# Another order for the first two tiles' work, half of each weight guard from VectorE's maxima, and the third tile transposed by DMA

## The chip, the cores and the metric

The kernel runs on one core of a Trainium2 chip. The metric is the device time of one execution in microseconds; the median of the runs counts. TensorE multiplies matrices, VectorE, ScalarE and GpSimd (POOL in the rows) do the elementwise work, and SyncE (SP) issues most DMA transfers.

## What is computed

One layer of an encoder on 4096 tokens of width 1024. The input is normalized, projected to eight groups of 512 columns (four for a gated convolution; q, k, v and a gate z for dilated window attention with eight heads), and the joined result goes through an output projection:

```python
h = rmsnorm(x, norm_w)
proj = jnp.einsum('bsd,de->bse', h, w_in)            # (4096 x 1024) @ (1024 x 4096)
u, g_b, g_c, z_conv, q, k, v, z_attn = jnp.split(proj, splits, axis=-1)
y_conv = short_gated_conv(u, g_b, g_c, conv_w, conv_b) * jax.nn.silu(z_conv)
q, k = rmsnorm(q, q_norm_w), rmsnorm(k, k_norm_w)    # per head of 64
for window, dilation in ((128, 1), (512, 4), (2048, 16)):
    o_i, lse_i = dilated_window_attention(q, k, v, rel_bias, window, dilation)
y_attn = sum(softmax(lses) * outs) * jax.nn.silu(z_attn)
x = x + jnp.concatenate([y_conv, y_attn], -1) @ w_out
```

## The kernel before

Every float32 operand of a product is split into two float16 parts, hi and lo, and a product is three matmuls (hi by hi, hi by lo, lo by hi) of 128 x 512 outputs. The program is written for each engine as one queue, in the order of the code; each engine works its queue strictly from front to back and waits where an operand is late.

The kernel has three phases: projections of q, k, v and z for all 32 tiles of 128 tokens (phase A), attention interleaved with the convolution's projections (phase B), and the output projection. The change touches the head of phase A only.

**Weights.** Groups 4, 5, 6 and 7 of `w_in` are q, k, v and z. A group is eight pieces of 128 x 512 (`raw`), one per 128 rows, called kt 0 to 7. Before it can be split, a group needs a scale that keeps its float16 parts in range, its guard. `w_square` sums a piece's squares on ScalarE into one column of `wss`; `w_scale` adds the eight columns, adds over the partitions by a one-column matmul with `ones` on TensorE, takes the inverse root on GpSimd and writes the scales `nws` on VectorE. Then `w_split` writes hi on ScalarE and lo on VectorE, piece by piece, to `wa`.

**Tiles.** `stats1` and `stats2` give a tile's inverse root of the mean square (ScalarE's sum, GpSimd's power, a few one-column steps on VectorE). Tiles 0, 1 and 2 go through `x_transpose`: VectorE scales the tile, TensorE transposes it in eight blocks to two banks of PSUM, ScalarE writes hi and VectorE lo. From tile 3 on `x_split` writes the two parts untransposed, and two DMA transposes from SyncE's queue bring them to `hb`.

**Products.** `mm` runs one group for one tile or, for the first two tiles, for both together, 48 matmuls; its argument `between` names work that is queued behind the matmuls of a kt. In the head the calls are pq, pk, pv and pz (groups 4 to 7 for tiles 0 and 1), and between their matmuls stand the next group's guard and splits, the norms of q and k (`post_qk1` sums squares, `post_qk2` scales and splits), and `v_sums`: eight matmuls with `ones16` over the absolute values of v's hi weights, which give per-column scales that `post_v` and `post_z` need. After pz the steady loop starts with group 4 of tile 2, here called pq(2).

Of the kernel before, what the change touches and what calls it, by code (L numbers as in the profile page):

```python
# [65 lines left out]
def tile_hybrid_block(  # L66
# [193 lines left out]
    def w_scale(cg):  # L260
# [28 lines left out]
    def group_steps(cg):  # L289
        def spl(kt):  # L290
            w = wa[(cg - 4) * 8 + kt]
            w_split(w[:, 0], w[:, 1], raw.pop((cg, kt)), cg, kt)
        return ([lambda kt=kt: w_square(cg, kt, raw[cg, kt]) for kt in range(KT)], [lambda: w_scale(cg)],
                [lambda kt=kt: spl(kt) for kt in range(KT)])
# [49 lines left out]
    def h_views(t):  # L344
        c = t // 2
        b = (hb[c] if t % 2 else h_room(c, c % 3))[:, t % 2]
        HT[t] = (b[:, 0], b[:, 1])
        return HT[t]

    def x_transpose(t, b0=4):  # L350
        hi, lo = h_views(t)
        nc.vector.tensor_scalar(XT[t], XT[t], RX.pop(t), None, op0=OP.mult)
        for g in range(2):
            p = bank(b0 + g, [128, 4, 128])
            for k in range(4):
# [91 lines left out]

    def v_sums():
        pcs = bank(7, [128, 512])
        for n in range(KT):  # L450
            a = pa.tile([128, 512], F16, name="wk", bufs=3)
            nc.scalar.activation(a, wa[16 + n][:, 0], AF.Abs)
            nc.tensor.matmul(pcs, ones16, a, start=n == 0, stop=n == KT - 1)
        nc.vector.tensor_scalar(vinv, pcs, 1e-30, None, op0=OP.max)
# [54 lines left out]
    steps = {cg: group_steps(cg) for cg in (4, 5, 6, 7)}  # L509
# [3 lines left out]
    stats1(0)  # L513
    stats1(1)
    stats2(0)
    stats2(1)
    x_transpose(0, 4)
    x_transpose(1, 6)
    for part in steps[4]:
        run_tasks(part)  # L520

    def with_steps(cg, more=None):
        sq, fin, spl = steps[cg]
        out = {kt: [] for kt in range(KT)}
        for kt in range(4):
            out[kt] += sq[2 * kt:2 * kt + 2]
        out[3] += fin
        for kt in range(4):
            out[4 + kt] += spl[2 * kt:2 * kt + 2]
        for kt, tasks in (more or {}).items():  # L530
            out[kt] += tasks
        return out

    pq = mm((0, 1), 0, 4, with_steps(5), 4)
    pk = mm((0, 1), 2, 5, with_steps(6, {
        0: [lambda: post_qk1(0, "q", pq[0])], 1: [lambda: post_qk1(1, "q", pq[1])], 2: [gains],
        5: [lambda: post_qk2(0, "q")], 7: [lambda: post_qk2(1, "q")]}))
    pv = mm((0, 1), 4, 6, with_steps(7, {
        0: [lambda: post_qk1(0, "k", pk[0]), lambda: qk_store(0, "q")], 1: [lambda: post_qk1(1, "k", pk[1])],
        2: [lambda: qk_store(1, "q"), v_sums], 3: [lambda: stats1(2)], 4: [v_scales, lambda: stats2(2)],  # L540
        5: [lambda: post_qk2(0, "k"), lambda: x_transpose(2, 0)], 6: [lambda: post_qk2(1, "k")], 7: [v_gate]}))
    load_x(3)
    load_x(4)
    pz = mm((0, 1), 2, 7, {
        0: [lambda: qk_store(0, "k"), lambda: post_v(0, pv[0])], 1: [lambda: qk_store(1, "k"), lambda: post_v(1, pv[1])],
        2: [lambda: h_store(0), lambda: stats1(3)], 4: [lambda: stats2(3)]})
# [704 lines left out]
```

## Time and profile before

| what | value |
|---|---|
| median of 3 runs | 2262.62 us (2255.15 to 2264.13) |
| the profiled execution's own time | 2264.64 us |
| its span | 2262.8 us |
| TensorE busy | 2152.2 us, 95% of the span |
| VectorE, ScalarE, GpSimd busy | 1427.5, 1087.2, 769.4 us |

The span is the time from the first to the last instruction in the trace; the execution's own time is 1.8 us longer. Times in the rows below are counted from the span's start.

### The profile page before, as it was taken

How to read it: one execution, taken by the hardware profiler on the slowest of the kernel's cores; microseconds unless marked ns; L12 is line 12 of the kernel's file. 1: busy time of each engine (PE TensorE's matmuls, PEld its weight loads, DVE VectorE, ACT ScalarE, POOL GpSimd, SP SyncE). 2: the span in 40 equal slices, each digit the busy share in tenths (PEclk: the TensorE clock that was granted, in tenths of full speed). 3: DMA queues.
4: the chain of work that ended last, by engine and by line, in shares of the span. 5: the costliest groups of instructions: out<-in, count | busy, mean ns of one | idle time of the engine just before them, and what ended most of it. 6: DMA issues, size and time to landing. Idle time of an engine off the chain costs nothing. (4 is left out here: it accounts for less than half of the span.)

```text
span 2262.8 us, 48552 instructions
## 1 busy us (share of the span) xinstructions
PE 2152.2 (95%) x17726; PEld 1577.9 (70%) x17726; DVE 1427.5 (63%) x4009; ACT 1087.2 (48%) x3128; POOL 769.4 (34%) x1443
## 2 busy tenths in 40 slices
PE   5699999999999989999999999999999998999999
PEld 2244444444444778888888888888888897788887
DVE  4655665656656356766566666676666676787776
ACT  6423333333333156766566666666566675222221
POOL 1132332222233134533344323553233254343332
PEclk9899999999999999999999999999999999999999
DMA  5246467685655775689565896668966558587775
GB/s 178 77 133 169 151 169 171 171 202 144 165 164 142 176 149 134 139 168 191 135 153 116 177 183 153 143 157 170 177 149 132 134 116 223 188 258 257 237 239 188
DMA packets 625005, 377.83 MB, mean 167 GB/s; under 512 B 401281, under 2 KB 567292, under 8 KB 618620
## 3 DMA queue, kind: packets, MB, share of 16 engines
q1 hardware_dynamic: 503396, 304.19, 54.3%
q10 hardware_dynamic: 121368, 70.53, 12.2%
q8 instruction: 139, 2.28, 0.4%
q14 instruction: 102, 0.84, 0.1%
HBM read 174.54 MB, written 110.39 MB: 126 GB/s over the span
## 5 line engine op out<-in xcount | busy, mean ns | idle before, releaser
L809 PE MATMUL bank<-hb,w 128*128 128x256 f16 x2048 | 562.9, 275 | 0.1
L810 PE MATMUL bank<-hb,w 128*128 128x256 f16 x2048 | 560.2, 274 | 0.0
L811 PE MATMUL bank<-hb,w 128*128 128x256 f16 x2048 | 560.1, 274 | 0.0
L998 DVE CUSTOM_DVE_ANT_0 L<-bank,bt,alpha 128x256 f32<-128x256 f32 (+1 forms) x768 | 318.9, 452 | 135.3 <-PE bank L986 89.7
L387 PE MATMUL bank<-wa,hb 128*128 128x512 f16 x1024 | 392.0, 383 | 5.8 <-DMA hb<-xs 5.8
L385 PE MATMUL bank<-wa,hb 128*128 128x512 f16 x1024 | 392.8, 384 | 2.1 <-ACT wa L286 2.1
L386 PE MATMUL bank<-wa,hb 128*128 128x512 f16 x1024 | 392.2, 383 | 0.2 <-DVE wa L287 0.2
L1007 ACT ACTIVATE L<-L,ot 128x256 f32<-128x256 f32 (+1 forms) x768 | 363.6, 476 | 25.8 <-DVE ot L998 23.4
L973 POOL COPY qz<-qk 64x128 f16<-64x128 f16 x512 | 155.3, 303 | 250.9 <-PE bank L986 229.3
L810 PEld LDWEIGHTS <-w 128*128 128x128 f16 x2048 | 203.4, 99 | 29.8 <-issue 0.2
L809 PEld LDWEIGHTS <-w 128*128 128x128 f16 x2048 | 203.4, 99 | 27.4
L811 PEld LDWEIGHTS <-w 128*128 128x128 f16 x2048 | 200.9, 98 | 24.4
L986 PE MATMUL bank<-qk,qz 128*128 128x256 f16 (+1 forms) x768 | 213.3, 298 | 0.0
L238 POOL TENSOR_TENSOR rs_rq<-rs_mq,mhalf 128x8 f32<-128x8 f32 x64 | 107.8, 1684 | 302.9 <-DVE rs_mq L237 302.9
L1042 DVE SCALAR_TENSOR_TENSOR pt<-bank,pt 128x512 f16<-128x512 f32 x192 | 132.5, 690 | 121.6 <-ACT pt L1030 121.0
L1030 ACT ACTIVATE pt<-bank 128x512 f16<-128x512 f32 x192 | 114.6, 597 | 186.4 <-PE bank L1024 181.5
L387 PEld LDWEIGHTS <-hb 128*128 128x128 f16 x1024 | 101.1, 99 | 132.5 <-DMA hb<-xs 9.2
L1061 PE MATMUL bank<-vt,pt 128*128 128x64 f16 x1536 | 175.8, 194 | 14.0 <-DMA pt<-src 9.1
L385 PEld LDWEIGHTS <-hb 128*128 128x128 f16 x1024 | 101.9, 99 | 123.5 <-issue 7.0
L386 PEld LDWEIGHTS <-hb 128*128 128x128 f16 x1024 | 101.1, 99 | 123.8 <-issue 6.3
L1046 DVE SCALAR_TENSOR_TENSOR src<-L,src 128x384 f16<-128x384 f32 (+1 forms) x192 | 127.9, 666 | 90.0 <-ACT src L1036 84.0
L1062 PE MATMUL bank<-vt,pt 128*128 128x64 f16 x1536 | 176.0, 194 | 0.0
(194 smaller groups left out, 4430.9 us busy)
## 6 DMA issues: line engine op xcount, KB each, us to landing
hb<-hT SPq DMA_DIRECT2D x32, 1024.0 KB, 5.8
o_d<-ot ACTq DMA_DIRECT2D x32, 528.0 KB, 5.2
qk<-o_d SPq DMA_DIRECT2D x63, 264.0 KB, 3.7
hT<-hb SPq DMA_DIRECT2D x16, 1024.0 KB, 4.1
wst<-in_w_in_dram SPq DMA_DIRECT2D x64, 256.0 KB, 2.8
qk<-in_x_dram SPq DMA_DIRECT2D x32, 512.0 KB
qk_d<-h SPq DMA_DIRECT2D x128, 96.0 KB, 3.3
vt<-v_d ACTq DMA_DIRECT2D x48, 256.0 KB, 4.0
```

The lines of the kernel that those rows point to most:

```text
L385: nc.tensor.matmul(p, hi[:, kt, :], w[:, 0], start=kt == 0, stop=False)
L386: nc.tensor.matmul(p, hi[:, kt, :], w[:, 1], start=False, stop=False)
L387: nc.tensor.matmul(p, lo[:, kt, :], w[:, 0], start=False, stop=kt == KT - 1)
L809: nc.tensor.matmul(pt, w_h, hi[:, :, kt], start=kt == 0, stop=False)
L810: nc.tensor.matmul(pt, w_h, lo[:, :, kt], start=False, stop=False)
L811: nc.tensor.matmul(pt, w_l, hi[:, :, kt], start=False, stop=kt == KT - 1)
L973: nc.gpsimd.tensor_copy(QZ[u % QZB][i][half], cols(q_t[i], U["qc"], half))
L986: nc.tensor.matmul(p[i][:, 0:kn], QZ[u % QZB][i], cols(qk_t[4], kc), start=False, stop=True)
L998: nc.vector.tensor_tensor_reduce(out=L[:, i], in0=p[i][:, 0:kn], in1=bias[:, U["b0"]:U["b0"] + kn], scale=alpha, scalar=BIG, op0=OP.add, o ...
L1007: nc.scalar.activation(L[:, i], L[:, i], AF.Exp, scale=-1.0, bias=ot[:, b, i, DH:DH + 1], accum_out=ot[:, b, i, DH + 1:DH + 2])
L1061: nc.tensor.matmul(p[:, i], hi, v[:, 0:DH], start=j == 0, stop=False)
L1062: nc.tensor.matmul(p[:, i], hi, v[:, DH:], start=False, stop=False)
```

## The change

Five things change, all in the code that runs before the steady loop.

1. The two tiles' preparation is reordered: tile 0 is scaled and transposed before VectorE takes up tile 1's sum, and `x_transpose` is cut in two, the transposes themselves and `x_parts`, which writes hi and lo.
2. Half of each guard comes from VectorE: `square` sums the squares of pieces 0 to 3 on ScalarE and lets `w_max` take the largest absolute value per partition of pieces 4 to 7 on VectorE; `w_scale` multiplies these four columns by the norm's weights and squares them (two more small steps). The convolution's groups keep eight sums of squares.
3. Guards run further ahead: part of group 5's guard stands before and between group 4's splits, group 6's in pq, group 7's in pk. Splits are spread over kt 3 to 7 of the call before.
4. The absolute values for `v_sums` are written by `v_abs` to eight buffers of their own at kt 6 of pv, and the eight matmuls stand between pv and pz instead of at kt 2 of pv. `v_scales`, `post_v` and `v_gate` stand in pz, which writes to banks 6 and 7.
5. Tile 2 goes through `x_split` and two DMA transposes at kt 7 of pv instead of through `x_transpose` at kt 5. The loads of tiles 3 and 4 come behind them on SyncE's queue.

```diff
--- before.py
+++ after.py
@@ -257,7 +257,16 @@
         sq = pa.tile([128, D], F16, name="xsq")[:, 0:512]
         nc.scalar.activation(sq, src, AF.Square, scale=nwc[:, kt:kt + 1], accum_out=wss[:, cg, kt:kt + 1])
 
-    def w_scale(cg):
+
+
+    def w_max(cg, kt, src):
+        nc.vector.tensor_reduce(wss[:, cg, kt:kt + 1], src, axis=AX.X, op=OP.max, apply_absolute_value=True)
+
+    def w_scale(cg, maxima=0):
+        if maxima:
+            t = wss[:, cg, KT - maxima:]
+            nc.vector.tensor_tensor(t, t, nwc[:, KT - maxima:], op=OP.mult)
+            nc.vector.tensor_tensor(t, t, t, op=OP.mult)
         tot = pa.tile([128, 2], F32, name="wtot", bufs=2)
         nc.vector.tensor_reduce(tot[:, 0:1], wss[:, cg], axis=AX.X, op=OP.add)
         p = bank(7, [128, 512])
@@ -286,12 +295,13 @@
         nc.scalar.activation(hi, src, AF.Copy, scale=s)
         nc.vector.scalar_tensor_tensor(lo, src, s, hi, op0=OP.mult, op1=OP.subtract)
 
-    def group_steps(cg):
-        def spl(kt):
-            w = wa[(cg - 4) * 8 + kt]
-            w_split(w[:, 0], w[:, 1], raw.pop((cg, kt)), cg, kt)
-        return ([lambda kt=kt: w_square(cg, kt, raw[cg, kt]) for kt in range(KT)], [lambda: w_scale(cg)],
-                [lambda kt=kt: spl(kt) for kt in range(KT)])
+    def spl(cg, kt):
+        w = wa[(cg - 4) * 8 + kt]
+        w_split(w[:, 0], w[:, 1], raw.pop((cg, kt)), cg, kt)
+
+    def square(cg, n):
+        w_square(cg, n, raw[cg, n])
+        w_max(cg, n + 4, raw[cg, n + 4])
 
 
 
@@ -348,13 +358,19 @@
         return HT[t]
 
     def x_transpose(t, b0=4):
-        hi, lo = h_views(t)
         nc.vector.tensor_scalar(XT[t], XT[t], RX.pop(t), None, op0=OP.mult)
+        out = []
         for g in range(2):
             p = bank(b0 + g, [128, 4, 128])
             for k in range(4):
                 kt = 4 * g + k
                 nc.tensor.transpose(p[:, k, :], XT[t][:, kt * 128:(kt + 1) * 128], identf)
+            out.append(p)
+        return out
+
+    def x_parts(t, banks):
+        hi, lo = h_views(t)
+        for g, p in enumerate(banks):
             s = slice(4 * g, 4 * g + 4)
             nc.scalar.activation(hi[:, s], p, AF.Copy)
             nc.vector.tensor_tensor(lo[:, s], p, hi[:, s], op=OP.subtract)
@@ -445,12 +461,18 @@
 
     vs = pa.tile([128, 512], F32, name="vs")
 
+    VA = []
+
+    def v_abs():
+
+        for n in range(KT):
+            VA.append(wpool.tile([128, 512], F16, name=f"w{n}"))
+            nc.scalar.activation(VA[n], wa[16 + n][:, 0], AF.Abs)
+
     def v_sums():
-        pcs = bank(7, [128, 512])
+        pcs = bank(2, [128, 512])
         for n in range(KT):
-            a = pa.tile([128, 512], F16, name="wk", bufs=3)
-            nc.scalar.activation(a, wa[16 + n][:, 0], AF.Abs)
-            nc.tensor.matmul(pcs, ones16, a, start=n == 0, stop=n == KT - 1)
+            nc.tensor.matmul(pcs, ones16, VA[n], start=n == 0, stop=n == KT - 1)
         nc.vector.tensor_scalar(vinv, pcs, 1e-30, None, op0=OP.max)
 
     def v_scales():
@@ -506,44 +528,52 @@
         nc.vector.tensor_scalar(cvec, cq[:, 2, :], cm[:, 1:2], QK_SCALE, op0=OP.mult, op1=OP.mult)
 
 
-    steps = {cg: group_steps(cg) for cg in (4, 5, 6, 7)}
     cq = pa.tile([128, 3, DH], F32, name="cq")
     nc.sync.dma_start(cq[:, 0, :], dap(q_norm_w, 0, [[0, 128], [1, DH]]))
     nc.sync.dma_start(cq[:, 1, :], dap(k_norm_w, 0, [[0, 128], [1, DH]]))
     stats1(0)
+    stats2(0)
+    xp0 = x_transpose(0, 4)
     stats1(1)
-    stats2(0)
+    x_parts(0, xp0)
     stats2(1)
-    x_transpose(0, 4)
-    x_transpose(1, 6)
-    for part in steps[4]:
-        run_tasks(part)
-
-    def with_steps(cg, more=None):
-        sq, fin, spl = steps[cg]
-        out = {kt: [] for kt in range(KT)}
-        for kt in range(4):
-            out[kt] += sq[2 * kt:2 * kt + 2]
-        out[3] += fin
-        for kt in range(4):
-            out[4 + kt] += spl[2 * kt:2 * kt + 2]
-        for kt, tasks in (more or {}).items():
-            out[kt] += tasks
-        return out
-
-    pq = mm((0, 1), 0, 4, with_steps(5), 4)
-    pk = mm((0, 1), 2, 5, with_steps(6, {
-        0: [lambda: post_qk1(0, "q", pq[0])], 1: [lambda: post_qk1(1, "q", pq[1])], 2: [gains],
-        5: [lambda: post_qk2(0, "q")], 7: [lambda: post_qk2(1, "q")]}))
-    pv = mm((0, 1), 4, 6, with_steps(7, {
-        0: [lambda: post_qk1(0, "k", pk[0]), lambda: qk_store(0, "q")], 1: [lambda: post_qk1(1, "k", pk[1])],
-        2: [lambda: qk_store(1, "q"), v_sums], 3: [lambda: stats1(2)], 4: [v_scales, lambda: stats2(2)],
-        5: [lambda: post_qk2(0, "k"), lambda: x_transpose(2, 0)], 6: [lambda: post_qk2(1, "k")], 7: [v_gate]}))
+    xp1 = x_transpose(1, 6)
+    for n in range(4):
+        square(4, n)
+        if n == 1:
+            x_parts(1, xp1)
+    w_scale(4, 4)
+    for n in range(2):
+        square(5, n)
+
+    def each(f, *a):
+        return lambda: f(*a)
+
+    def spls(cg, *kts):
+        return [each(spl, cg, kt) for kt in kts]
+
+    for kt in range(KT):
+        spl(4, kt)
+        if kt in (1, 2):
+            square(5, kt + 1)
+    pq = mm((0, 1), 0, 4, {
+        0: [each(w_scale, 5, 4)], 1: [each(square, 6, 0), each(square, 6, 1)], 2: [each(square, 6, 2), each(square, 6, 3)],
+        3: spls(5, 0, 1), 4: spls(5, 2, 3), 5: spls(5, 4, 5), 6: spls(5, 6, 7)})
+    pk = mm((0, 1), 2, 5, {
+        0: [each(w_scale, 6, 4)], 1: [each(square, 7, 0), each(square, 7, 1), gains], 2: [each(square, 7, 2), each(square, 7, 3)],
+        3: [each(post_qk1, 0, "q", pq[0])] + spls(6, 0, 1), 4: spls(6, 2, 3), 5: [each(post_qk1, 1, "q", pq[1])] + spls(6, 4),
+        6: spls(6, 5, 6) + [each(post_qk2, 0, "q")], 7: spls(6, 7) + [each(post_qk2, 1, "q")]})
+    pv = mm((0, 1), 4, 6, {
+        0: [each(w_scale, 7, 4), each(qk_store, 0, "q")], 1: [each(post_qk1, 0, "k", pk[0]), each(qk_store, 1, "q")],
+        2: spls(7, 0, 1), 3: spls(7, 2, 3) + [each(post_qk1, 1, "k", pk[1])], 4: spls(7, 4, 5),
+        5: spls(7, 6, 7) + [each(stats1, 2)], 6: [each(post_qk2, 0, "k"), v_abs, each(stats2, 2)],
+        7: [each(post_qk2, 1, "k"), each(x_split, 2)]})
+    v_sums()
     load_x(3)
     load_x(4)
-    pz = mm((0, 1), 2, 7, {
-        0: [lambda: qk_store(0, "k"), lambda: post_v(0, pv[0])], 1: [lambda: qk_store(1, "k"), lambda: post_v(1, pv[1])],
-        2: [lambda: h_store(0), lambda: stats1(3)], 4: [lambda: stats2(3)]})
+    pz = mm((0, 1), 6, 7, {
+        0: [each(qk_store, 0, "k"), each(qk_store, 1, "k")], 1: [v_scales, each(post_v, 0, pv[0])], 2: [each(stats1, 3)],
+        3: [each(post_v, 1, pv[1])], 5: [each(stats2, 3), v_gate], 7: [each(h_store, 0)]})
     tw = conv_w_tasks()
     per = -(-len(tw) // (NT - 6))
     pq = mm((2,), 0, 4)[0]
```

Where the queues differ, at three places.

VectorE's queue at the start, before: from the first tile's sum to the first group's scale. `rs_mx` and `rs_rx` are a tile's sum and inverse root, `xt` and `hb_144` the raw tiles 0 and 1, `hb_255` the transposed parts, `wss` the guard's columns.

```order
L247 TENSOR_TENSOR rs_rx<-rs_rx,rs_t_245 128x1
L244 TENSOR_TENSOR rs_t_250<-rs_rx 128x1
L245 TENSOR_TENSOR rs_t_250<-rs_t_250,rs_mx 128x1
L246 TENSOR_SCALAR rs_t_250<-rs_t_250 128x1
L247 TENSOR_TENSOR rs_rx<-rs_rx,rs_t_250 128x1
L352 TENSOR_SCALAR xt<-xt,rs_rx 128x1024
L360 TENSOR_TENSOR hb_255<-bank_257,hb_255 128x512
L360 TENSOR_TENSOR hb_255<-bank_264,hb_255 128x512
L352 TENSOR_SCALAR hb_144<-hb_144,rs_rx 128x1024
L360 TENSOR_TENSOR hb_255<-bank_272,hb_255 128x512
L360 TENSOR_TENSOR hb_255<-bank_279,hb_255 128x512
L262 TENSOR_REDUCE wtot<-wss 128x1
```

The same place after the change:

```order
L361 TENSOR_SCALAR xt<-xt,rs_rx 128x1024
L237 TENSOR_SCALAR rs_mx<-ssx 128x1
L376 TENSOR_TENSOR hb_261<-bank_244,hb_261 128x512
L376 TENSOR_TENSOR hb_261<-bank_249,hb_261 128x512
L244 TENSOR_TENSOR rs_t_266<-rs_rx 128x1
L245 TENSOR_TENSOR rs_t_266<-rs_t_266,rs_mx 128x1
L246 TENSOR_SCALAR rs_t_266<-rs_t_266 128x1
L247 TENSOR_TENSOR rs_rx<-rs_rx,rs_t_266 128x1
L361 TENSOR_SCALAR hb_144<-hb_144,rs_rx 128x1024
L263 TENSOR_REDUCE wss<-w_158 128x1
L263 TENSOR_REDUCE wss<-w_160 128x1
L376 TENSOR_TENSOR hb_261<-bank_272,hb_261 128x512
```

Tile 0's scaling (`xt`) moved ahead of tile 1's sum, and maxima of the first group's pieces (`wss<-w`) now stand between the two tiles' parts.

TensorE's queue where the `ones16` matmuls over v's weights begin, before (`wa_125` to `wa_132` are v's split pieces 0 to 7, bank_566 is pv of tile 1):

```order
L386 LDWEIGHTS hb_255
L386 MATMUL bank_566<-wa_127,hb_255 128x512
L387 LDWEIGHTS hb_255
L387 MATMUL bank_566<-wa_127,hb_255 128x512
L453 LDWEIGHTS ones_220
L453 MATMUL bank_621<-wk,ones_220 128x512
```

and after (pv of tile 1 is bank_572):

```order
L402 LDWEIGHTS hb_261
L402 MATMUL bank_572<-wa_132,hb_261 128x512
L403 LDWEIGHTS hb_261
L403 MATMUL bank_572<-wa_132,hb_261 128x512
L475 LDWEIGHTS ones_220
L475 MATMUL bank_731<-w_686,ones_220 128x512
```

The eight matmuls moved from behind v's piece 2 to behind its last piece, so that thirty more matmuls of pv stand ahead of them; tile 2's eight transposes, which stood on this queue behind piece 5, are gone.

SyncE's queue between the constants and the results of the first two tiles, before (`qk_d<-h` stores q and k, `xt` and `hb_144` are the loads of tiles 3 and 4, `v_d` stores v):

```order
L512 DMA cq<-in_k_norm_w_dram 128x64
L427 DMA qk_d<-h_531 128x1x256 x4
L427 DMA qk_d<-h_562 128x1x256 x4
L204 DMA xt<-in_x_dram 128x1024
L204 DMA hb_144<-in_x_dram 128x1024
L427 DMA qk_d<-h_709 128x1x384 x4
L436 DMA v_d<-h_776 128x1024
```

and after (`hb_728` is tile 2's transposed half):

```order
L533 DMA cq<-in_k_norm_w_dram 128x64
L443 DMA qk_d<-h_549 128x1x256 x4
L443 DMA qk_d<-h_568 128x1x256 x4
L385 DMA_TRANSPOSE hb_728<-xs_724 128x8x128
L385 DMA_TRANSPOSE hb_728<-xs_725 128x8x128
L204 DMA xt<-in_x_dram 128x1024
L204 DMA hb_144<-in_x_dram 128x1024
L443 DMA qk_d<-h_682 128x1x384 x4
L443 DMA qk_d<-h_720 128x1x384 x4
```

Tile 2's two DMA transposes now stand behind q's eight stores, and the loads of tiles 3 and 4 moved behind the transposes.

## Rows read from the trace of the kernel before

**Rows 1.** The page: the span, and the first line of its part 1 (busy time, share of the span, instructions).

```profile
span 2262.8 us, 48552 instructions
...
PE 2152.2 (95%) x17726; PEld 1577.9 (70%) x17726; DVE 1427.5 (63%) x4009; ACT 1087.2 (48%) x3128; POOL 769.4 (34%) x1443
```

**Rows 2.** The chain of waits on TensorE over the whole span: the waiting instruction, whom it waited for, us in total, times, longest.

```profile
PE bank L264 <- DVE wtot L262: 22.4, 7, 7.6
PE bank L1024 <- ACT L L1007: 22.0, 25, 2.9
PE bank L357 <- DVE hb L352: 12.6, 2, 10.6
PE bank L453 <- ACT wk L452: 11.1, 1, 11.1
...
PE bank L387 <- DMA hb<-xs: 5.8, 6, 1.9
```

**Rows 3.** Busy time by stage: for each stretch its length, each engine's busy time and instructions, the granted clock of TensorE, the DMA engines' share and GB/s.

```profile
0.00:26.00 26.00, 4.50 (x18) 3.67 (x19) 6.62 (x23) 12.37 (x25) 2.12 (x8) 1.00 0.95 335
26.00:45.00 19.00, 14.62 (x49) 5.67 (x49) 11.80 (x31) 16.53 (x33) 0.55 (x1) 0.91 0.20 71
45.00:67.00 22.00, 15.11 (x71) 6.71 (x69) 15.34 (x41) 13.44 (x29) 3.85 (x3) 0.98 0.04 13
67.00:93.00 26.00, 9.31 (x33) 3.64 (x33) 14.33 (x31) 15.39 (x33) 5.52 (x5) 0.70 0.16 54
93.00:107.90 14.90, 14.90 (x64) 6.83 (x63) 10.57 (x22) 6.57 (x11) 1.68 (x2) 0.87 0.18 61
107.90:200.00 92.10, 92.10 (x428) 41.75 (x427) 48.29 (x111) 28.91 (x48) 28.86 (x23) 1.00 0.55 160
```

**Rows 4.** The timeline of TensorE in the head: start, length, engine, instruction, and in brackets the idle time before it and what ended it.

```profile
38.19 0.38 PE L264 MATMUL bank<-wtot,ones 128*128 128x1 f32 x2 [3.10 <-DVE wtot L262]
...
73.05 4.01 PE L453 MATMUL bank<-wk,ones 128*128 128x512 f16 x8 [11.13 <-ACT wk L452]
...
91.99 1.97 PE L357 MATMUL bank<-identf,hb 128*128 128x128 f32 x8 [10.56 <-DVE hb L352]
```

**Rows 5.** The timeline of all engines up to the first group's splits (columns as in rows 4; x8 are eight merged instructions).

```profile
5.79 0.57 POOL L238 TENSOR_TENSOR rs_rx<-rs_mx,mhalf 128x1 f32<-128x1 f32 x1 [4.72 <-DVE rs_mx L237]
...
8.61 0.15 DVE L244 TENSOR_TENSOR rs_t<-rs_rx 128x1 f32<-128x1 f32 x1
...
10.02 0.75 DVE L352 TENSOR_SCALAR xt<-xt,rs_rx 128x1024 f32<-128x1024 f32 x1
...
17.37 0.71 ACT L258 ACTIVATE xsq<-w,nwc 128x512 f16<-128x512 f32 x1
...
24.13 0.16 DVE L262 TENSOR_REDUCE wtot<-wss 128x1 f32<-128x8 f32 x1 [5.93 <-ACT xsq L258]
...
26.30 5.01 ACT L286 ACTIVATE wa<-w,nws 128x512 f16<-128x512 f32 x8 [2.21 <-DVE nws L269]
...
27.06 5.39 DVE L287 SCALAR_TENSOR_TENSOR wa<-w,nws,wa 128x512 f16<-128x512 f32 x8 [0.17 <-ACT wa L286]
```

**Rows 6.** The timeline of VectorE from 46 to 90 us: the instructions that give prices, and those that bound a block (L401 a sum over heads, L262 the first step of a scale, L287 splits, L244 the first step of `post_qk2`, L457 a reciprocal).

```profile
46.96 0.69 DVE L401 TENSOR_REDUCE ssq<-wk 128x8 f32<-128x512 f32 x1 [0.93 <-ACT wk L399]
47.68 0.23 DVE L237 TENSOR_SCALAR rs_mq<-ssq,rqs 128x8 f32<-128x8 f32 x1
...
49.85 0.22 DVE L498 SCALAR_TENSOR_TENSOR cq<-cq 128x64 f32<-128x64 f32 x1
...
51.06 0.25 DVE L506 TENSOR_SCALAR cvec<-cq,cm 128x64 f32<-128x64 f32 x1
52.23 0.16 DVE L262 TENSOR_REDUCE wtot<-wss 128x1 f32<-128x8 f32 x1 [0.92 <-ACT xsq L258]
...
54.91 2.74 DVE L287 SCALAR_TENSOR_TENSOR wa<-w,nws,wa 128x512 f16<-128x512 f32 x4 [0.54 <-ACT wa L286]
57.56 0.16 DVE L244 TENSOR_TENSOR rs_t<-rs_rq 128x8 f32<-128x8 f32 x1
...
61.21 2.74 DVE L287 SCALAR_TENSOR_TENSOR wa<-w,nws,wa 128x512 f16<-128x512 f32 x4
...
82.22 3.35 DVE L457 RECIPROCAL vs<-vinv 128x512 f32<-128x512 f32 x1
...
87.92 0.16 DVE L244 TENSOR_TENSOR rs_t<-rs_rq 128x8 f32<-128x8 f32 x1
...
88.84 0.69 DVE L409 TENSOR_TENSOR wk<-bank,rs_rq 128x512 f32<-128x512 f32 x1
```

**Rows 7.** The timeline of ScalarE: the absolute values, a hi part of k, and the first sum of squares behind pq(2).

```profile
72.38 4.25 ACT L452 ACTIVATE wk<-wa 128x512 f16<-128x512 f16 x8
...
89.57 0.63 ACT L416 ACTIVATE h<-wk 128x512 f16<-128x512 f32 x1 [6.88 <-DVE wk L409]
...
113.69 0.60 ACT L399 ACTIVATE wk<-bank 128x512 f32<-128x512 f32 x1 [4.43 <-PE bank L387]
```

**Rows 8.** The DMA transposes: the issues of 100 to 300 us (count, median us from issue to landing), and the first pair on SyncE's queue.

```profile
hb<-xs SPq DMA_TRANSPOSE x18, 3.9
...
115.34 2.77 SPq L369 DMA_TRANSPOSE hb<-xs  x2
```

**Rows 9.** TensorE alone in the 3.4 us behind the wait that ends at 38.19: length, busy time and instructions, granted clock, DMA share, GB/s.

```profile
39.00:42.40 3.40, 3.40 (x10) 0.50 0.00 0
```

## The prediction

> **What bounds the kernel now.** TensorE is busy for 2152.2 of the 2262.8 us [rows 1], so I looked first at what it waits for over the whole run, then at where. The waits [rows 2] that belong to the head by their lines are those for scales (L264), for tile scaling (L357) and for absolute values (L453). The stretches [rows 3] show the place: up to 93.0 us TensorE works 4.50 + 14.62 + 15.11 + 9.31 = 43.5 us and stands idle for the other 49.5; from 93.0 to 200 us it is never idle. So the head is bound by what feeds TensorE and the loop behind it by TensorE. Time taken from the head moves the whole loop forward, as long as the loop has no other bound.
>
> The end of the head is the start of pq(2). ScalarE's sum of squares at 113.69 us waits for the last matmul of pq(2) [rows 7]. A matmul in the loop takes 92.10 / 428 = 0.215 us [rows 3], pq(2) has 24 of them, 5.2 us, and some 0.2 us pass until ScalarE starts, so pq(2) starts at 113.69 - 5.4 = **108.3 us**. I work out when it starts after the change.
>
> The large waits inside the head [rows 4]: 11.13 us for the absolute values, which stand in ScalarE's queue behind v's last splits, the second norm of q and six squares, while TensorE holds the `ones16` matmuls ahead of ready work; and 10.56 us for tile 2's scaling on VectorE, which stands behind a reciprocal of 3.35 us and the norm of k [rows 6]. Both waits go, because the instruction that waits is moved or removed. They do not simply add up to a gain: what is late next is VectorE's own queue, which gets the maxima.
>
> **The first scale.** Before, tile 0's inverse root is ready at 5.79 + 0.57 = 6.4 us, yet its scaling starts at 10.02, behind tile 1's sum; the two sets of four small steps run from 8.61 to 10.02, 0.7 us each [rows 5]. After, tile 0 is scaled at 6.4 + 0.7 = 7.1, 2.9 us earlier. Tile 1 follows less early, since its four small steps come behind tile 0's parts: about 2.1 us, so its last hi part on ScalarE ends near 15.4 instead of 17.4, where the squares start [rows 5]. A square takes (24.13 - 17.37) / 8 = 0.845 us. Two squares fit between the tiles' parts, two remain: 15.4 + 1.7 = 17.1 us. VectorE in the same time writes tile 1's parts and four maxima and is done near 17.7. Two more small steps (0.38, at the 0.19 that such steps take) give 18.1 us where 24.13 stood. The way from there to the first hi split, 26.30 - 24.13 = 2.2 us, is unchanged: **20.3 us**, 6.0 us earlier.
>
> **VectorE's queue after that.** VectorE begins its part at about 20.9, behind the remaining small steps. From there to the scaled k of tile 0, on which ScalarE's next work hangs, its queue holds:
> - 32 lo splits, 5.39 / 8 = 0.674 us each [rows 5]: 21.6 us.
> - 12 of the 16 maxima. Before has none. The nearest row is the sum over 128 x 512 float32 on the same engine, 0.69 us [rows 6]; the farthest operation of that size in the head is the reciprocal, 3.35 us, and a bound below is half the row, 0.35. I take 0.69, since operation kind, elements and type agree: 8.3 us.
> - three scales, each as long as before from its first step to its first split, 54.91 - 52.23 = 2.7 us [rows 6], of which the wait for hi now covers the two new steps: 8.1 us.
> - four sums of a norm with their small step, 47.68 + 0.23 - 46.96 = 0.95 us: 3.8 us; the gains, 51.06 + 0.25 - 49.85 = 1.5 us [rows 6].
> - the two norms of q, 61.21 - 57.56 = 3.65 us each with the wait for ScalarE in them: 7.3 us; the first norm of k up to its product, 88.84 + 0.69 - 87.92 = 1.6 us [rows 6].
> - a wait at group 6's scale, whose matmul stands behind 48 matmuls. TensorE reaches these after an idle stretch of about 6 us. After one of 3.10 us [rows 4] the granted clock was 0.50, the 1.2 GHz level, for 3.4 us [rows 9], which costs 1.7 us of work. 48 x 0.215 + 1.7 = 12.0 us stand against 11 to 11.6 us of VectorE's work: 1 us, between 0 and 2.
>
> Sum: 21.6 + 8.3 + 8.1 + 3.8 + 1.5 + 7.3 + 1.6 + 1.0 = 53.2; VectorE reaches that point at 20.9 + 53.2 = **74.1 us**. ScalarE has 12 squares (10.1) and 32 splits of 5.01 / 8 = 0.626 us (20.0) in the same stretch and waits for VectorE, not the other way.
>
> **From there to pq(2).** ScalarE writes k's hi part (0.63, [rows 7]) and then the eight absolute values, 4.25 us [rows 7]: 79.0 us. The `ones16` matmuls follow one by one and end near 79.5. pv's other 42 matmuls were released by z's scale, near 64, and take 9.0 us plus 1.7 for a half clock after the idle stretch ahead of them, so they end near 75 and cost nothing. pz is 48 x 0.215 = 10.3 us, its weights long split: pq(2) could start at **89.8 us**, 18.5 us earlier than 108.3.
>
> **The third tile.** The eight transposes and the scaling leave TensorE's and VectorE's queues; x_split adds one instruction on ScalarE and one on VectorE, behind k's second norm, then two transposes on SyncE. hi is written near 81 us, lo near 82.2. q's stores stand ahead in that queue but end before 70. A transpose lands 3.9 us after its issue (median, [rows 8]): 86 us, needed at 89.8. Hidden with 3.7 us to spare; every microsecond beyond costs one. The loads of tiles 3 and 4 come behind them, near 84, and are first used near 88 and later, beside pz and pq(2).
>
> This is the place where a rule of the Trainium skill speaks against the change. "VectorE: DVE Perf Modes", section "Rules for kernel authors", sends a 128 x 128 transpose to TensorE if PSUM will do and to the DMA otherwise, and its section "The three transpose paths" gives 390 ns against 1309 ns a block. Read as a price per block, the tile's 16 blocks would be an estimated 21 us, and pq(2) would begin near 102 us instead of 89.8. No row here bears that reading out: the transposes in the loop, eight blocks each, land 3.9 us after their issue [rows 8].
>
> `v_scales`, `post_v` and `v_gate` move beside pz, 10 us in which VectorE has about that much work; their first reader is `post_z`, behind pz. Nothing on TensorE waits for them before tile 3.
>
> **The sum.** The profiled execution took 2264.64 us, 1.8 us of it outside the span. Less 18.5 it is 2246.1 us. The median of the runs shown is 2.0 us below that execution, so I forecast **2244 us** for the median, 0.8% faster. 0.5%, 11.3 us, is about what a measurement of this kernel can tell from no change.
>
> **Rivals.**
> - *Half of it is given back in the loop.* For: the loop waits for transposes too, 5.8 us in six waits [rows 2], and other DMA work could fall differently beside them. Against: 107.9 to 200 us shows no idle time at all [rows 3], and the later waits hang on the order of work, which is kept, not on the clock. 9 us given back: 2253 us.
> - *Tile 2's transposes land late.* If the second takes as long as the whole of pz and more, say 21 us from the first issue near 81, pq(2) starts near 102: a gain of 6.5 us, 2256 us. For: TensorE has waited for such transposes in the loop [rows 2], where they are issued some 13 us ahead (115.34 us [rows 8], against 108.3 + 96 x 0.215 = 128.9). Against: before them the DMA engines have almost nothing to do (a share of 0.04 to 0.16 from 45 to 93 us, [rows 3]).
> - *The maxima are slow, and the kernel gets slower.* Twelve maxima stand on VectorE's path and two more on the way to the first scale, so each microsecond above 0.69 costs 14. The gain is gone at 0.69 + 18.5 / 14 = 2.0 us a maximum. At the reciprocal's 3.35 us it is 14 x 2.66 = 37 us, 18.7 us slower than before: 2281 us. For: no row shows a maximum with absolute values. Against: the sum at 0.69 is the same kind of instruction.
>
> **Chances and range.** Forecast 0.72, with a range of its own from 2235 to 2251: below, maxima at 0.35 (14 x 0.34 = 4.8 us) and the spread of the runs, about 4 us; above, 2 us for pz's first matmuls at half clock, 1 us at group 6's scale and the same spread. Given back 0.12, transposes late 0.10, maxima slow 0.04, the rest unknown. The range for 8 in 10 takes in the second and third case: 2235 to 2256. Faster by over 0.5% means below 2251.3: nearly all of the forecast and a third of the two cases next to it, 0.77; within 0.5% 0.17; slower 0.06.
>
> **What would show it.** Right: the first hi split near 20 us, maxima of 0.7 us, VectorE almost without idle time from 20 to 75 us, no wait of 10 us on TensorE for absolute values or for tile 2, one of about 10 us for z's scale in their place, and pq(2) near 90 us. Wrong: maxima over 1 us, a wait of pq(2) for `hb`, or a gap between pq(2)'s gain and the end's. It fails most easily in VectorE's sum, where 53 us rest on prices from a stretch that was less full.

## The result and the profile after

The changed kernel takes **2239.92 us** (median of four, 2236.22 to 2241.75) against 2260.5 us for the kernel before on the same chip: a ratio of **0.9909**, 95% interval 0.9882 to 0.9935. Timed again beside other kernels it gave 0.9919 (0.9905 to 0.9933). It is faster by 0.8 to 0.9%.

The page after (before: [rows 1]), and the waits of TensorE over the whole span, columns as in [rows 2]:

```profile
span 2239.8 us, 48497 instructions
...
PE 2148.0 (96%) x17718; PEld 1576.5 (70%) x17718; DVE 1438.3 (64%) x4031; ACT 1074.5 (48%) x3095; POOL 771.3 (34%) x1443
```

```profile
PE bank L273 <- DVE wtot L271: 27.0, 7, 9.7
PE bank L1054 <- ACT L L1037: 25.2, 23, 4.5
PE bank L367 <- DVE xt L361: 7.9, 1, 7.9
...
PE bank L403 <- DMA hb<-xs: 5.0, 5, 1.9
...
PE bank L367 <- DVE hb L361: 2.8, 1, 2.8
```

and of the kernel before, tile 0's own scaling, which [rows 2] leaves out:

```profile
PE bank L357 <- DVE xt L352: 10.8, 1, 10.8
```

TensorE's work is the same to 0.2%; its idle time fell from 110.6 to 91.8 us. The wait for absolute values (11.1) is gone, that for tile scaling fell from 12.6 to 2.8, tile 0's own from 10.8 to 7.9, and the waits for scales rose from 22.4 to 27.0: -11.1 - 9.8 - 2.9 + 4.6 = -19.2 us. The attention's waits (L1054) and those for the loop's transposes (L403) stayed within the spread that all traces of this case show, 21.9 to 27.8 and 4.5 to 6.6 us. By stage, columns as in [rows 3]:

```profile
0.00:26.00 26.00, 7.37 (x24) 4.31 (x24) 15.74 (x44) 16.68 (x33) 2.12 (x8) 1.00 0.95 337
26.00:45.00 19.00, 16.28 (x68) 7.43 (x69) 14.20 (x40) 14.22 (x30) 1.10 (x2) 1.00 0.20 69
45.00:67.00 22.00, 12.26 (x47) 5.16 (x46) 18.53 (x48) 8.53 (x15) 6.61 (x4) 0.77 0.08 24
67.00:90.00 23.00, 21.93 (x97) 9.34 (x96) 17.13 (x32) 11.40 (x20) 5.63 (x6) 1.00 0.37 98
90.00:110.00 20.00, 20.00 (x94) 9.02 (x93) 12.96 (x30) 6.31 (x10) 8.39 (x6) 1.00 0.55 177
```

Before, TensorE stood still for 16.7 us of 67 to 93; now it is busy from 67 on but for 1.1 us. The last long idle time lies in 45 to 67, where VectorE is the fullest engine, with 18.53 of 22 us. The timeline along the head's path (columns as in [rows 4]):

```profile
19.94 1.33 ACT L295 ACTIVATE wa<-w,nws 128x512 f16<-128x512 f32 x2 [1.35 <-DVE nws L278]
...
20.45 1.27 DVE L263 TENSOR_REDUCE wss<-w 128x1 f32<-128x512 f32 x2
...
31.12 2.45 DVE L263 TENSOR_REDUCE wss<-w 128x1 f32<-128x512 f32 x4
33.50 5.38 DVE L296 SCALAR_TENSOR_TENSOR wa<-w,nws,wa 128x512 f16<-128x512 f32 x8
...
41.76 0.16 DVE L274 TENSOR_SCALAR wtot<-bank 128x1 f32<-128x1 f32 x1 [2.42 <-PE bank L273]
...
61.85 0.59 PE L273 MATMUL bank<-wtot,ones 128*128 128x1 f32 x2 [9.74 <-DVE wtot L271]
...
72.08 0.69 DVE L425 TENSOR_TENSOR wk<-bank,rs_rq 128x512 f32<-128x512 f32 x1
...
73.34 4.25 ACT L470 ACTIVATE w<-wa 128x512 f16<-128x512 f16 x8
...
74.00 4.01 PE L475 MATMUL bank<-w,ones 128*128 128x512 f16 x8
...
79.17 2.72 SPq L385 DMA_TRANSPOSE hb<-xs  x2
...
93.59 0.60 ACT L415 ACTIVATE wk<-bank 128x512 f32<-128x512 f32 x1 [1.29 <-PE bank L403]
```

The last row is the first sum of squares behind pq(2) (113.69 before, [rows 7]). By the prediction's working, pq(2) starts at 93.59 - 5.4 = **88.2 us**; pz, at 78.0 + 10.3 = 88.3, says the same, and so does a count: behind the four calls of 48 matmuls the next one starts at 88.21 (before: 108.31). Before it was 108.3, so the head is 20.1 us shorter. In the experiments this start is read in the same way unless said otherwise.

### The profile page after: what moved, and what is told of

It reads as the page before. It is cut to its first block, busy times and chain, and to the rows that moved or that the text cites. A ratio compares the mean times of both kernels' runs of the same rounds, so it can differ in the third digit from the quotient of the medians.

```text
span 2239.8 us, 48497 instructions
## 1 busy us (share of the span) xinstructions
PE 2148.0 (96%) x17718; PEld 1576.5 (70%) x17718; DVE 1438.3 (64%) x4031; ACT 1074.5 (48%) x3095; POOL 771.3 (34%) x1443
## 3 DMA queue, kind: packets, MB, share of 16 engines
q10 hardware_dynamic: 121368, 70.53, 12.1%
## 5 line engine op out<-in xcount | busy, mean ns | idle before, releaser
L403 PE MATMUL bank<-wa,hb 128*128 128x512 f16 x1024 | 392.1, 383 | 5.0 <-DMA hb<-xs 5.0
L401 PE MATMUL bank<-wa,hb 128*128 128x512 f16 x1024 | 391.9, 383 | 2.6 <-ACT wa L295 2.1
L403 PEld LDWEIGHTS <-hb 128*128 128x128 f16 x1024 | 101.0, 99 | 131.5 <-DMA hb<-xs 7.5
L401 PEld LDWEIGHTS <-hb 128*128 128x128 f16 x1024 | 102.1, 100 | 125.0 <-issue 6.5
```

What stands on the lines that cost most here:

```text
L401: nc.tensor.matmul(p, hi[:, kt, :], w[:, 0], start=kt == 0, stop=False)
L403: nc.tensor.matmul(p, lo[:, kt, :], w[:, 0], start=False, stop=kt == KT - 1)
```

## The experiments

**The parts alone.** Three kernels put one part each into the kernel before. First the sums (part 4 of the change):

```diff
-        2: [lambda: qk_store(1, "q"), v_sums], 3: [lambda: stats1(2)], 4: [v_scales, lambda: stats2(2)],
+        2: [lambda: qk_store(1, "q")], 3: [lambda: stats1(2)], 4: [lambda: stats2(2)],
...
+    v_sums()
...
-        0: [lambda: qk_store(0, "k"), lambda: post_v(0, pv[0])], 1: [lambda: qk_store(1, "k"), lambda: post_v(1, pv[1])],
+        0: [lambda: qk_store(0, "k")], 1: [v_scales, lambda: post_v(0, pv[0]), lambda: qk_store(1, "k")],
...
```

> The kernel before with one part of the change alone: the absolute values and their eight matmuls moved from kt 2 of pv to behind pv, the reciprocal and post_v into pz. Theory A (queues): the wait of 11.1 us on TensorE goes, but z's scale still needs ScalarE's eight squares of z, which end near 78.2 - 4.25 = 74 us, tile 2's scaling on VectorE still stands behind z's splits and k's norm, and the absolute values now come behind all of ScalarE's splits, so the time is spent again in waits for z's scale, for tile 2 and for the absolute values: pq(2) starts at 107 us instead of 108.3, within 2 us. Theory B (each wait counts by itself): 11.1 us less, pq(2) at 97 us.

One execution took 2256.56 us (before on that chip 2258.91), and pq(2) starts at 112.93 - 5.4 = 107.5: 0.8 us earlier. TensorE's waits in that head:

```profile
74.65 0.59 PE L264 MATMUL bank<-wtot,ones 128*128 128x1 f32 x2 [11.21 <-DVE wtot L262]
...
84.69 1.97 PE L357 MATMUL bank<-identf,hb 128*128 128x128 f32 x8 [4.53 <-DVE hb L352]
...
93.34 4.01 PE L453 MATMUL bank<-wk,ones 128*128 128x512 f16 x8 [2.35 <-ACT wk L452]
```

The 11.13 us of [rows 4] did not go, they took another name: z's scale, next on the queue, now waits 11.21 us. That is Theory A (107 us; B said 97).

Then tile 2's transposes by DMA (part 5), in place of `x_transpose`:

```diff
-        5: [lambda: post_qk2(0, "k"), lambda: x_transpose(2, 0)], 6: [lambda: post_qk2(1, "k")], 7: [v_gate]}))
+        5: [lambda: post_qk2(0, "k"), lambda: x_split(2)], 6: [lambda: post_qk2(1, "k")], 7: [v_gate]}))
```

> The kernel before with another part alone: tile 2 through x_split and two DMA transposes at kt 5 of pv instead of through TensorE. Theory A: TensorE no longer stands at 81.4 us for tile 2's scaling, but v's and z's remaining matmuls wait for VectorE's queue, which still holds the reciprocal, k's norms and z's splits; what VectorE saves is the scaling (0.75) and two lo parts less one of 1.28: pq(2) at 107.5 us, within 1.5 us. Theory B: 10.6 us of wait and 2 us of transposes less, pq(2) at 96 us.

One execution took 2263.92 us, above all nine of the kernel before on that chip (2257.60 to 2262.72), though pq(2) starts at 113.16 - 5.4 = 107.8, 0.5 us earlier. Single executions spread too far to tell such a head; this is why the start is read. TensorE's waits:

```profile
73.70 4.22 PE L453 MATMUL bank<-wk,ones 128*128 128x512 f16 x8 [11.14 <-ACT wk L452]
...
90.75 0.61 PE L385 MATMUL bank<-wa,hb 128*128 128x512 f16 x1 [5.57 <-DVE wk L409]
...
96.63 0.59 PE L385 MATMUL bank<-wa,hb 128*128 128x512 f16 x1 [4.41 <-DVE wk L409]
```

The 10.56 us for tile 2 come back as 5.57 + 4.41: pz writes to banks 2 and 3, which hold pk until `post_qk2` of k has read them (L409), once for each tile. The start is where Theory A put it (107.5; B said 96), by a wait that neither it nor the prediction named.

Then the maxima (part 2), four of eight pieces of each group, with `w_max` and `w_scale` as in the change:

```diff
...
-        return ([lambda kt=kt: w_square(cg, kt, raw[cg, kt]) for kt in range(KT)], [lambda: w_scale(cg)],
+        return ([lambda kt=kt: (w_max if kt > 3 else w_square)(cg, kt, raw[cg, kt]) for kt in (0, 4, 1, 5, 2, 6, 3, 7)], [lambda: w_scale(cg, 4)],
```

> The kernel before with a third part alone: maxima on VectorE for pieces 4 to 7 of the four guards, nothing else moved. Theory A: each guard before holds VectorE until ScalarE's eighth square, since the old order puts nothing of VectorE's beside them; four squares less are 3.4 us a guard for the four guards, of which the maxima stand beside the squares: 9 us less, pq(2) at 99 us, within 2 us, and a time ratio of 0.996. Theory B (the maxima are cheap but ScalarE is not the bound, VectorE is): 16 x 0.6 = 9.6 us more on VectorE, pq(2) between 105 and 112 us, no gain.

2251.55 us (six runs), ratio 0.9966 (0.9953 to 0.9978), and pq(2) at 106.66 - 5.4 = 101.3: 7.0 us earlier, 2.3 us short of A's 99 and outside B's 105 to 112.

```profile
64.88 4.22 PE L460 MATMUL bank<-wk,ones 128*128 128x512 f16 x8 [5.83 <-ACT wk L459]
...
84.70 1.97 PE L364 MATMUL bank<-identf,hb 128*128 128x128 f32 x8 [10.57 <-DVE hb L359]
```

ScalarE, freed of half its squares, has the absolute values ready some 8 us sooner (64.88 against 73.05); tile 2's wait stays. Together the three parts alone give 0.8 + 0.5 + 7.0 = 8.3 of the 20.1 us.

**The parts taken out of the changed kernel.** Without the maxima, all squares on ScalarE:

```diff
-        w_max(cg, n + 4, raw[cg, n + 4])
+        w_square(cg, n + 4, raw[cg, n + 4])
...
```

(the calls of `w_scale` lose their 4 with it)

> The changed kernel with the maxima undone: all eight pieces of a guard by squares on ScalarE, the new order kept. Theory A: in the new order the guards run a group ahead, so the squares lie beside VectorE's splits and only the first guard, whose squares end 3.4 us later, and a little of the others show, while VectorE has 9.6 us less: pq(2) at 90.5 us against 88.2, so the maxima are worth 2 to 3 us here where they are worth 9 alone. Theory B: the maxima are worth the same as in the old order, pq(2) at 97 us. Theory C (VectorE's sum alone decides): 9.6 us less on VectorE, pq(2) at 79 to 82 us.

2241.57 us. The first sum of squares, at 94.88, waits for VectorE here and not for TensorE, so I take pq(2) from the end of the sums (below): 75.29 + 4.01 + 10.3 = 89.6, 1.4 us later. That is Theory A, which said 2 to 3 us; B's 97 and C's 79 to 82 are out.

```profile
18.89 0.56 PE L273 MATMUL bank<-wtot,ones 128*128 128x1 f32 x2 [4.21 <-DVE wtot L271]
...
31.05 0.59 PE L273 MATMUL bank<-wtot,ones 128*128 128x1 f32 x2 [5.37 <-DVE wtot L271]
...
44.34 0.28 PE L273 MATMUL bank<-wtot,ones 128*128 128x1 f32 x2
...
63.13 0.59 PE L273 MATMUL bank<-wtot,ones 128*128 128x1 f32 x2 [8.13 <-DVE wtot L271]
...
75.29 4.01 PE L475 MATMUL bank<-w,ones 128*128 128x512 f16 x8 [0.67 <-ACT w L470]
```

Worth 7.0 us in the old order, the maxima are worth 1.4 in the new one. Without them the first three scales come 0.8, 2.3 and 2.9 us later than in the changed kernel (18.07, 28.72 and 41.45 there), but z's, the fourth, only 1.3 (61.85): on the way to z's scale VectorE, which has no maxima to take there, makes good 1.6 us, and ScalarE, busy for 8.53 of the 22 us from 45 to 67 in the changed kernel, had room for the squares. So the maxima help the early guards and cost something at z's. And with each maximum done twice:

```diff
-        nc.vector.tensor_reduce(wss[:, cg, kt:kt + 1], src, axis=AX.X, op=OP.max, apply_absolute_value=True)
+        for _ in range(2):
+            nc.vector.tensor_reduce(wss[:, cg, kt:kt + 1], src, axis=AX.X, op=OP.max, apply_absolute_value=True)
```

> The changed kernel with every maximum taken twice: 16 x 0.6 us more on VectorE, nothing else. Theory A (VectorE's queue is the path of the changed head): 14 of the 16 stand on it, less about 1 us that the wait at group 6's scale gives back: pq(2) at 95.7 us against 88.3, within 1 us. Theory B (ScalarE's or TensorE's queue is the path): pq(2) below 90 us.

2251.10 us, pq(2) at 102.05 - 5.4 = 96.65, 8.4 us later, 14 us for each microsecond that a maximum (0.60) gets longer. VectorE's queue is the path (Theory A, which said 95.7; B said below 90).

The sums put back to kt 2 of pv (bank 7), with the absolute values ahead of them:

```diff
-        2: spls(7, 0, 1), 3: spls(7, 2, 3) + [each(post_qk1, 1, "k", pk[1])], 4: spls(7, 4, 5),
+        2: [v_abs, v_sums] + spls(7, 0, 1), 3: spls(7, 2, 3) + [each(post_qk1, 1, "k", pk[1])], 4: spls(7, 4, 5),
...
-    v_sums()
...
```

> The changed kernel with the absolute values and their matmuls back at kt 2 of pv, as before the change, all else new. Theory A: in the new order TensorE waits there for z's scale anyway and ScalarE has time, so the wait of 11 us does not come back; what ends last is then tile 2's transposes or z's splits: pq(2) at 87.5 us, within 1.5 us of 88.3. Theory B (the move of the matmuls is worth its own wait): pq(2) at 97 us or later.

2240.72 us, and pq(2) loses nothing: it starts at 86.5 and, with its second wait, runs as if from 87.3, where Theory A said 87.5 and B 97. The weight loads of pq(2) show what ends last then, tile 2's transposes, issued 4 us later at 83.11:

```profile
86.49 0.10 PEld L401 LDWEIGHTS <-hb 128*128 128x128 f16 x1 [1.22 <-DMA hb<-xs]
87.77 0.10 PEld L403 LDWEIGHTS <-hb 128*128 128x128 f16 x1 [1.16 <-DMA hb<-xs]
```

So the move of the sums brings 0.8 us in the old order and nothing in the new one, where it costs some 0.9. Tile 2 by TensorE again, at kt 7 of pv:

```diff
-        7: [each(post_qk2, 1, "k"), each(x_split, 2)]})
+        7: [each(post_qk2, 1, "k"), lambda: x_parts(2, x_transpose(2, 0))]})
```

> The changed kernel with tile 2 again transposed by TensorE, at the same place of the code (kt 7 of pv). Theory A: the eight transposes stand ahead of the matmuls of the absolute values and of pz, and wait for tile 2's scaling behind k's second norm on VectorE, which is only written near 79.5 us; transposes (2.0 us), the absolute values' matmuls and pz follow at the lower clock at first: pq(2) at 95 us against 88.3, within 1.5 us. Theory B (only the work of the transposes counts): 2 us, pq(2) at 90.3 us.

pq(2) at 101.41 - 5.4 = 96.0, 7.8 us later (Theory A said 95), since the transposes, which stand between pv and the sums, wait for the tile's scaling behind k's second norm:

```profile
80.55 1.97 PE L367 MATMUL bank<-identf,hb 128*128 128x128 f32 x8 [5.63 <-DVE hb L361]
```

Worth 0.5 us in the old order, the DMA path is worth 7.8 in the new one. But the one execution took 2242.48 us, only 1.3 to 2.6 us more than the changed kernel's medians. Whether the loop gives head time back is the question of the last experiments.

`x_split` delayed to kt 5 of pz measures the transposes themselves:

```diff
-        7: [each(post_qk2, 1, "k"), each(x_split, 2)]})
+        7: [each(post_qk2, 1, "k")]})
...
+        3: [each(post_v, 1, pv[1])], 5: [each(stats2, 3), v_gate, each(x_split, 2), each(load_x, 4)], 7: [each(h_store, 0)]})
```

> The changed kernel with tile 2's x_split moved to kt 5 of pz, so that pq(2) has to wait for the two DMA transposes and the wait's end shows when they land. The issues come near 89 us (hi) and 91 us (lo). By the rows of the loop, 3.9 us from issue to landing: pq(2) starts near 93.5 us and its third matmul waits for lo until 95.5 or 96. By a price per block of 1.3 us (the page's figure): eight blocks, 10.5 us for hi and as much again for lo: pq(2) near 99.5 us, its third matmul near 110.

2248.95 us. TensorE stands ready and waits for each half:

```profile
89.34 3.57 SPq L385 DMA_TRANSPOSE hb<-xs  x2
...
92.56 0.39 PE L401 MATMUL bank<-wa,hb 128*128 128x512 f16 x1 [3.28 <-DMA hb<-xs]
...
94.75 0.61 PE L403 MATMUL bank<-wa,hb 128*128 128x512 f16 x1 [1.59 <-DMA hb<-xs]
...
102.23 0.60 ACT L415 ACTIVATE wk<-bank 128x512 f32<-128x512 f32 x1 [11.88 <-PE bank L403]
```

The first half lands 3.2 us after its issue, the second within 2.2 us of the first: the size that the rows of the loop gave, and a third or less of the 10.5 us a half that the expectation estimates from a price per block. pq(2) then ran slower than usual (last section), so that its end is late by 8.6 us.

**Does the end keep what the head gains?** The changed kernel and the one with tile 2 on TensorE, timed five times each, and two kernels that shorten the head further. "v's scale" in these expectations is the last group's, z's; "tile 0's absolute values" are those of v's weights; and the third tile's transposes stand at kt 7 of pv, as above, not of pk.

> The changed kernel itself, timed again beside the two that follow on the same chip. Both theories: ratio to the kernel before near 0.991 (about 2240 us), start of tile 2's group 4 near 88.2 us.

> The changed kernel with its third tile transposed by TensorE at group 7 of p·k, whose single look had the head 7.7 us longer and the time only some 2.6 us longer. Theory A (what the head loses, the end loses: nothing behind it has slack): 7.7 us over the changed kernel of this call, ratio to the kernel before 0.9943. Theory B (two thirds of it is given back behind the head, as the single look reads): 2 to 3 us over it, ratio 0.992. Between the two a part is given back.

Timed again, the changed kernel's pq(2) starts at 93.83 - 5.4 = 88.4, and with tile 2 on TensorE at 101.59 - 5.4 = 96.2: the starts repeat within 0.3 us. One kernel has the absolute values at kt 6 and 7 of pk (`v_abs` takes the numbers of the pieces):

```diff
-        6: spls(6, 5, 6) + [each(post_qk2, 0, "q")], 7: spls(6, 7) + [each(post_qk2, 1, "q")]})
+        6: spls(6, 5, 6) + [each(v_abs, *range(7)), each(post_qk2, 0, "q")], 7: spls(6, 7) + [each(v_abs, 7), each(post_qk2, 1, "q")]})
...
-        5: spls(7, 6, 7) + [each(stats1, 2)], 6: [each(post_qk2, 0, "k"), v_abs, each(stats2, 2)],
+        5: spls(7, 6, 7) + [each(stats1, 2)], 6: [each(post_qk2, 0, "k"), each(stats2, 2)],
```

> Only tile 0's absolute values are taken earlier on ScalarE (seven of the eight pieces behind p·k's sixth group, the last one behind its seventh). Theory A (the 4.3 us from scaled k over the absolute values to the matmuls of sums lie on the path): the path from k's product at 72.8 loses the absolute values, and what ends last is then v's scale with p·v and the sums behind it, group 4 of tile 2 near 85.5 instead of 88.2. Theory B (they lie beside other work): 88.2.

The other has these too, takes z's guard wholly by squares (the False) and puts the gains ahead of the scale that they stood behind:

```diff
-        0: [each(w_scale, 6, 4)], 1: [each(square, 7, 0), each(square, 7, 1), gains], 2: [each(square, 7, 2), each(square, 7, 3)],
+        0: [gains, each(w_scale, 6, 4)], 1: [each(square, 7, 0, False), each(square, 7, 1, False)], 2: [each(square, 7, 2, False), each(square, 7, 3, False)],
...
-        0: [each(w_scale, 7, 4), each(qk_store, 0, "q")], 1: [each(post_qk1, 0, "k", pk[0]), each(qk_store, 1, "q")],
+        0: [each(w_scale, 7), each(qk_store, 0, "q")], 1: [each(post_qk1, 0, "k", pk[0]), each(qk_store, 1, "q")],
```

> VectorE's queue made shorter by 3.8 us: the last weight group's guard comes from squares on ScalarE alone (four maxima at 0.60 gone), the gains (1.4) go ahead of v's scale's wait, and tile 0's absolute values are taken piece by piece behind each norm product. Theory A (VectorE's queue is what ends last before v's scale): v's scale on TensorE near 58.0 instead of 61.85, tile 2's group 4 near 81.3 instead of 88.2, ratio near 0.988. Theory B (another queue ends as late: ScalarE's, or tile 2's DMA transposes, whose first half landed by about 85): group 4 at 86 or later, ratio 0.990 to 0.991.

With the absolute values early, the eight matmuls take 1.89 us instead of 4.01:

```profile
74.23 1.89 PE L475 MATMUL bank<-w,ones 128*128 128x512 f16 x8
```

pq(2) starts at 91.70 - 5.4 = 86.3, 1.9 us earlier: the absolute values lie on the path (Theory A, which said 85.5; B said 88.2). Only so much, since pv itself, behind z's scale at 62.1, ends at 74.2. Its one execution, 2245.16 us, lies above the changed kernel's runs (2238.38 to 2241.32) in spite of that; why is not shown, but the five runs with tile 2 on TensorE spread over 8 us, so one execution can't tell 1.9. The shorter VectorE queue moves z's scale, and with it all that follows on TensorE:

```profile
57.77 0.58 PE L273 MATMUL bank<-wtot,ones 128*128 128x1 f32 x2 [5.58 <-DVE wtot L271]
...
70.10 1.89 PE L475 MATMUL bank<-w,ones 128*128 128x512 f16 x8
...
87.56 0.60 ACT L415 ACTIVATE wk<-bank 128x512 f32<-128x512 f32 x1 [1.31 <-PE bank L403]
```

pq(2) starts at 82.2, 6.0 us earlier than in the changed kernel (A said 81.3; B 86 or later): 4.1 us by z's scale and 1.9 by the early absolute values. What the four maxima and the gains give each was not told apart. The time is **2234.67 us** (four runs), ratio 0.9889, below the changed kernel's. All kernels that were timed several times, against the kernel before; the last column is (1 - ratio) x 2258.6 us with its interval:

| kernel | head shorter | ratio (95%) | end earlier |
|---|---|---|---|
| before + maxima | 7.0 us | 0.9966 (0.9953 to 0.9978) | 7.7 us (5.0 to 10.6) |
| after, tile 2 on TensorE | 12.1 us | 0.9941 (0.9926 to 0.9955) | 13.3 us (10.2 to 16.7) |
| after, timed again | 19.9 us | 0.9919 (0.9905 to 0.9933) | 18.3 us (15.1 to 21.5) |
| after, less on VectorE | 26.1 us | 0.9889 (0.9875 to 0.9904) | 25.1 us (21.7 to 28.2) |

The end follows the head one for one in all four, within intervals of some 3 us either way. The 1.3 to 2.6 us above came from a single execution: by the medians of five, tile 2 on TensorE costs 4.6 us (A said 7.7, B 2 to 3), and the runs of the two kernels lie 0.8 to 11.6 us apart, so the direct comparison leaves both open. Its ratio to before, 0.9941, is where A put it (0.9943), and B's 0.992 is outside its interval; but B reckoned from 0.991 for the changed kernel, and from the 0.9919 measured here it would say 0.993, which is inside. What speaks for A is the whole table, in which no kernel's end falls short of its head by more than its interval.

## Why the prediction was right

The forecast was 2244 us; the time came 4.1 us lower. 1.6 us of that is the head (88.2 for 89.8); another 2.1 us is the reference, since the forecast set out from a median of 2262.62 us, which with a fourth run is 2260.5; the rest is small beside the spread of the runs.

- **The first scale.** 20.3 us to the first hi split; 19.94 measured.
- **VectorE's queue**, named as the weakest step, held: from 20.45 (20.9) over 52.3 us (53.2) to scaled k at 72.8 (74.1). Its terms missed on both sides. A maximum takes 0.60 us in a series, (33.50 - 31.12) / 4, not 0.69: 1.2 us less. The three scales with the wait at group 6's took 10.2 us for 9.1: VectorE had only 10.0 us of work beside the 48 matmuls where 11 to 11.6 was reckoned, so that it waited 2.42 us. The sums of the norms came 0.4 us lower, the splits also. That these misses add up to no more than 0.9 us is in part luck. The sign that was named, one wait of about 10 us for z's scale, came with 9.74. That the queue is on the path was argued; the doubled maxima show it, at the slope of 14 that the third rival used.
- **From there to pq(2).** k's hi part, 4.25 us of absolute values, the sums, 10.3 us of pz: measured as written. The half clock behind the wait took 2.4 us from pv and not 1.7 (twelve matmuls from 62.30 to 67.30, 5.0 us where 2.6 is usual). One claim was too loose, that pv "costs nothing": it ended only 2 us ahead of the path, and that is why early absolute values bring 1.9 us and not 4.3.
- **Tile 2.** Hidden, as said. The row of the loop (3.9 us a half) was the better guide than the reading per block of the Trainium skill's "VectorE: DVE Perf Modes", section "The three transpose paths" (390 against 1309 ns): with nothing to hide it a half of eight blocks landed in 3.2 us, where that reading makes an estimated 10.5. The preference for TensorE in the Trainium skill's "VectorE: DVE Perf Modes", section "Rules for kernel authors", read as a rule for this place, would have cost the head 7.8 us, most of it the 5.6 of waiting for the scaling and the 2.0 of the transposes.
- **"Both waits go."** True of the whole change, and the reason given, that the waiting instruction is moved or removed, was not enough. In the old order that alone brings 0.8 and 0.5 us. The prediction did ask what is late next, and answered with VectorE's queue, which holds in the new order alone; it missed pz's banks altogether. The new kernel's pz uses banks 6 and 7. In the changed kernel k's products are done with banks 2 and 3 at 72.8 and 76.8, ahead of pz at 78.0, so the old banks might have done as well; a kernel with them was not tried.
- **Rivals.** No giving back in the loop shows (the table, within its intervals); pq(2) has no wait for tile 2's transposes; a maximum takes 0.60 us.

Where the gain comes from in the new order: it is not the sum of its parts. Alone in the old order the three parts bring 8.3 of the 20.1 us; taken out of the new one, each by itself, they cost 1.4 (the maxima), 7.8 (the DMA path) and nothing (the sums). Either way some 11 to 12 us are left that hang on the order, guards further ahead and tile 0 first, or on its play with the parts. To the order belongs a step that the list of the change leaves out: pq now alternates between the two tiles at every kt, where before it ran four kt of a tile at a time (the last argument of `mm`). No run tried the order by itself, so what each of its steps brings stays open.

## What to carry to other kernels

A wait on a strictly ordered queue is removed only if the next instruction's operand is early too: list what is late next on that queue, PSUM banks included, before its length is booked as a gain. Test a part both ways, alone in the old kernel and taken out of the new one; here the maxima went from 7.0 to 1.4 us and the DMA transposes from 0.5 to 7.8. And where a head feeds a bound loop, read its start and compare that: here it repeated within 0.3 us, where single executions of one kernel spread over as much as 8.

## What was not expected of the hardware

TensorE at half speed is not always seen in the granted clock. Behind the 9.74 us wait the changed kernel's clock reads 0.50, the 1.2 GHz level, and matmuls start every 0.43 us (the last two rows). Behind the 4.00 us wait that ends at 28.72 they also start 0.43 us apart, for 4 us, but the clock of that stretch reads 1.00; from 33.24 on they start 0.22 us apart:

```profile
31.25 0.63 PE L403 MATMUL bank<-wa,hb 128*128 128x512 f16 x1
31.68 0.63 PE L401 MATMUL bank<-wa,hb 128*128 128x512 f16 x1
...
34.75 0.38 PE L403 MATMUL bank<-wa,hb 128*128 128x512 f16 x1
34.97 0.38 PE L401 MATMUL bank<-wa,hb 128*128 128x512 f16 x1
...
63.10 0.63 PE L403 MATMUL bank<-wa,hb 128*128 128x512 f16 x1
63.53 0.63 PE L401 MATMUL bank<-wa,hb 128*128 128x512 f16 x1
```

The stretches, columns as in [rows 3]:

```profile
31.00:34.00 3.00, 3.00 (x11) 1.15 (x9) 3.00 (x8) 3.00 (x6) 0.00 (x0) 1.00 0.00 0
...
61.00:65.00 4.00, 3.15 (x9) 1.46 (x10) 2.44 (x13) 1.33 (x4) 0.56 (x1) 0.50 0.22 66
```

So I read the spacing of matmuls beside the clock; why the two differ stays open. With the late `x_split`, too, two short waits for data (3.28 and 1.59 us) were followed by 4 us at a granted clock of 0.50:

```profile
95.00:99.00 4.00, 4.00 (x11) 1.37 (x10) 0.00 (x0) 0.00 (x0) 0.00 (x0) 0.50 0.88 346
```
